# A two-layer hybrid diffusion step on one core: the first context pair's gate-up product moved to POOL, its down products placed ahead of the latent index list

## The chip, the cores and the metric

The kernel runs as one program on one core of a Trainium2 chip. The metric is device time in microseconds (us), median over runs. Engines: PE (TensorE, matmuls), DVE (VectorE), ACT (ScalarE), POOL (GpSimd) and SP (SyncE, which here only issues DMAs).

## The reference, cut to what matters

One step of a two-layer trunk for 128 context tokens and 512 latent tokens, model width 1024, float32. Each layer mixes tokens (attention, pooling, short convolution), adds a residual with a layer norm, and then runs a mixture of 16 experts of width 512, in which every expert picks its own tokens:

```python
def expert_choice_ffn(u, w_router, w_gate, w_up, w_down):
    B, T, D = u.shape
    cap = CAPACITY_FACTOR * T // N_EXPERTS
    aff = jax.nn.softmax((u @ w_router).astype(jnp.float32), axis=-1)
    g, idx = lax.top_k(aff.swapaxes(1, 2), cap)
    xs = jax.vmap(lambda ub, ib: ub[ib])(u, idx)
    hdn = (jax.nn.silu(jnp.einsum('becd,edf->becf', xs, w_gate))
           * jnp.einsum('becd,edf->becf', xs, w_up))
    ye = jnp.einsum('becf,efd->becd', hdn, w_down) * g[..., None].astype(u.dtype)
```

The two token sets are routed apart: an expert takes 16 of the 128 context tokens and 64 of the 512 latent ones. The rows of `ye` are then added back to their tokens.

## The kernel before, in words

The experts are worked in 8 pairs per layer (`NPAIR`). A pair has two kinds of rows: 2 x 16 context rows (in two blocks of 32) and 2 x 64 latent rows. Their products go into PSUM banks: `ps_gc` holds gate and up of the context rows, in four blocks of 32 partitions (gate and up of the first expert, gate and up of the second); `ps_g` and `ps_u` hold those of the latent rows; `ps_dc` and `ps_d` the down products.

A pair's context part is a chain: `context` (matmuls into `ps_gc`), `ctx_hidden` (ACT takes Silu of the gate block into `sc`, DVE multiplies it with the up block in PSUM into `hc`, once per expert), `ctx_turn` (PE transposes `hc` into `ps_hcT`, ACT copies that to `hcT`), `ctx_rows` (32 matmuls into `ps_dc`, then DVE scales the rows into `yc`), `scatter` (POOL adds `yc` to the accumulator `yaccc` by indirect DMA).

The first pair (j == 0) is special, since the latent tokens are not chosen yet when it begins. `route_late` finishes the router for the last latent tile with context matmuls filled in between (`fill`), picks the 64 best tokens per expert on DVE (`topk`: eight rounds of max, replace, find index), and builds the index list (`route_lat`): DVE writes `ldup`, PE transposes it (`tcol`, into `ps_tc`), DVE casts it to `lgi`, and POOL gathers the first pair's rows `xsl` from DRAM with `lgi` (`gather`). A second list, of the weights, goes the same way (`lvd`, `lg`). PE then transposes `xsl` (`turn_x`), ACT and DVE turn it into `xT`, and `ps_g`, `ps_u` follow.

The order of each engine's queue comes from a scheduler that emits instructions as it finds them ready. `tc.issue_after(x)` puts what follows behind `x` in that order; between engines it makes no wait at run time. `mm` and `turn1` chain most expert matmuls and transposes to each other in this way (`line["pe"]` is the last of them, line 239 issues them all). Before, the two DVE multiplies of the first pair's `ctx_hidden` were put behind the cast of `lgi`:

```python
scatter(yaccc, ctx_rows(ctx_turn(ctx_hidden(order["lgi"]))), csi, j)
```

Two more things hang on the gather. The weight tiles of 1 MB (`wg`, `wu`, `wd`) come through SP's queue into 16 buffers, refilled as PE frees them. Load number 13 (`GATE`, the tile `wg_3_0`) is held until POOL has written one element of its buffer, and that memset stands behind the first gather:

```python
if n == GATE:
    with tc.issue_after(order["gather"].ins):
        nc.gpsimd.memset(t[0:1, 0, 0:1], 0.0)
```

And POOL applies the layer norm's gain and bias to the latent residual tiles (lines 337 and 338, about 2.4 us each) and stores them to `yacc` (line 842); these stand in its queue around the gathers. The last 6 of the 96 weight tiles of a layer are paced: each waits until the one two places before it has landed (`PACED`, `PACE`).

Of the kernel before, what the change touches and what calls it, by code (L numbers as in the profile page):

```python
# [16 lines left out]
ALU = mybir.AluOpType  # L17
# [18 lines left out]
CAPL = 64  # L36
# [29 lines left out]
def kernel(ctx: ExitStack, tc: tile.TileContext, a: dict):  # L66
    nc = tc.nc
# [9 lines left out]
    order = {}  # L77
# [77 lines left out]
    yaccc = dram.tile([CROWS, EDIM], F32, name="yaccc")  # L155
# [78 lines left out]
    line = {}  # L234
# [541 lines left out]
    def out_proj(l, mixA, mixC, w2, ms, mixed):  # L776
# [170 lines left out]
        def route_late(fill):  # L947


            ins = turn(3, 1, fill(2), lambda ins: fill(1, ins))  # L950
            route(3, fill(1, ins))
            fill(9, order["weighed"])
            latr = route_lat(rt, rx, topk(rx, afl, CAPL, "ta"))
            order.pop("gather", None)
            x_first = gather(newrow("xsl"), zrow[:, :], latr[0][:, 0:1])
            cpool(f"rx{l}")
            return latr, x_first
# [98 lines left out]
    def experts(l, A, B, ctxr, ln, gates, newrow, newhalf, residual, xc, route_late, ps_dn, preload, start_next, finish, keep):  # L1056
# [68 lines left out]
        for j in range(NPAIR):  # L1125
# [34 lines left out]
            def ctx_hidden(after=None):  # L1160
                sc = newhalf("sc")
                hc = newhalf("hc")[0:64]
                for i in range(2):
                    nc.scalar.activation(out=sc[64 * i + 32:64 * i + 64], in_=pc[64 * i:64 * i + 32], func=AF.Silu)  # L1164
                    with tc.issue_after(after.ins) if after else ExitStack():
                        nc.vector.tensor_tensor(out=hc[32 * i:32 * i + 32], in0=pc[64 * i + 32:64 * i + 64],  # L1166
                                                in1=sc[64 * i + 32:64 * i + 64], op=ALU.mult)
                return hc
# [9 lines left out]
            def ctx_rows(hcT, pd=None):  # L1178
                if pd is None:
                    pd = ps_dn.tile("ps_dc")  # L1180
                for f in range(4):
                    for q in range(4):
                        i, n = q // 2, q % 2
                        mm(pd[32 * q:32 * q + 32, :], lhsT=hcT[:, f, 32 * i:32 * i + 32],
                           rhs=w["d", i, f // 2][:, f % 2, n * 512:n * 512 + 512], start=(f == 0), stop=(f == 3))
                yc = newhalf("yc") if j == NPAIR - 1 else wk.tile([P, 512], F32, tag="yc", name="yc", bufs=2)
# [33 lines left out]
            if j == 0:  # L1220
# [7 lines left out]
                (lgi, lso, lg, llast), x_first = route_late(fill)  # L1228
                xp = opool(f"xT{l}", "left")
                scatter(yaccc, ctx_rows(ctx_turn(ctx_hidden(order["lgi"]))), csi, j)  # L1230
# [320 lines left out]
```

## Time and profile before

| | |
|---|---|
| median of 3 runs | 1268.43 us (1268.24 to 1269.1) |
| profiled execution, its own time | 1264.65 us |
| its span in the trace | 1262.9 us |
| PE busy | 1180.2 us, 93% of the span |
| DVE, ACT, POOL busy | 542.2, 367.9, 252.6 us |
| mean DMA rate over the span | 271 GB/s |

Times in the trace count from the start of the span. Layer 0's selection of latent tokens lies at 349 to 361 us, its expert stage runs to about 640 us; layer 1's selection lies at 947 to 959 us. A timeline row gives start, duration, engine, line, operation, output and inputs, partitions x elements, count, and in brackets how long the engine was idle before and what ended that. A busy PE is one with a matmul in flight, at whichever of its two clocks (1.2 or 2.4 GHz); the granted clock is 0.5 or 1.0 in the rows by stretch.

### The profile page before, as it was taken

Reading aid. Unit: us, or ns where it says so; the run is one execution under the profiler, and the core shown is the slowest. Engines: PE = TensorE matmul, PEld = TensorE weight load, DVE = VectorE, ACT = ScalarE, POOL = GpSimd, SP = SyncE. Lnnn points to the kernel's source line nnn. Section 1 sums busy time; section 2 is a strip of 40 time slices with the busy share of each in tenths; the row PEclk is TensorE's granted clock in tenths of the full one; section 3 lists DMA queues with packets and bytes.
Section 4 is the critical chain, followed back from the end, with each engine's and each line's share of the span. In section 5 each row is a group of like instructions: output and inputs, shape, how many; then the busy total and the mean of one; then the engine's idle time right before and its main releaser. Section 6 shows DMA issues by size and latency. Waiting matters only on the chain.

```text
span 1262.9 us, 18196 instructions
## 1 busy us (share of the span) xinstructions
PE 1180.2 (93%) x7244; PEld 707.2 (56%) x7244; DVE 542.2 (43%) x1266; ACT 367.9 (29%) x800; POOL 252.6 (20%) x234
## 2 busy tenths in 40 slices
PE   5999999999959999999979999999996999999994
PEld 1877786987623333333349999698762333333331
DVE  1555454786551121111187656477644111111126
ACT  1532234672411111111155423466341111111111
POOL 0210001003241211112165100100324121112304
PEclk9999999999989999999989999999998999999997
DMA  9858674353869999999943324425396999999972
GB/s 365 309 205 315 220 268 175 127 175 135 328 235 404 402 397 409 408 407 362 327 142 96 78 60 201 168 100 194 132 341 236 402 399 402 410 408 406 358 252 84
DMA packets 85078, 342.34 MB, mean 271 GB/s; under 512 B 18713, under 2 KB 32089, under 8 KB 54401
## 3 DMA queue, kind: packets, MB, share of 16 engines
q1 hardware_dynamic: 73568, 305.96, 62.6%
q0 software_dynamic: 9840, 29.45, 8.5%
q10 hardware_dynamic: 1584, 5.77, 1.1%
q8 instruction: 57, 0.93, 0.3%
q14 instruction: 29, 0.23, 0.1%
HBM read 313.73 MB, written 27.51 MB: 270 GB/s over the span
## 4 chain that ended last, share of the span: by engine, by line
PE 83%; DVE 7%; DMA 4%; ACT 3%; issue 1%; SPq 0%; POOL 0%; POOLq 0%; ACTq 0%; DVEq 0%
PE ps_d L239 9%; PE ps_g L239 8%; PE ps_u L239 8%; PE ps_gc L239 8%; PE ps_dc L239 4%; PE ps_ada L185 4%; PE ps_c L230 3%; PE ps_c L232 3%; PE ps_c L231 3%; PE ps_o L231 3%; PE ps_o L230 3%; PE ps_o L232 3%; DMA r_wA<-in_w_in_dram 1%; PE tr L239 1%; PE ps_p L733 1%
## 5 line engine op out<-in xcount | busy, mean ns | idle before, releaser
L239 PE MATMUL ps_d<-wd,hT 128*64 128x512 f32 x512 | 114.9, 596 | 5.0 <-DVE yc L1187 3.2
L239 PE MATMUL ps_g<-wg,xT 128*64 128x512 f32 x512 | 116.1, 595 | 0.1
L239 PE MATMUL ps_u<-wu,xT 128*64 128x512 f32 x512 | 115.3, 592 | 0.0
L239 PE MATMUL ps_gc<-wu,xc 128*32 128x512 f32 x512 | 115.0, 594 | 0.0
L239 PE MATMUL ps_gc<-wg,xc 128*32 128x512 f32 x512 | 115.0, 594 | 0.0
L1164 ACT ACTIVATE sc<-ps_gc 32x512 f32<-32x512 f32 x32 | 18.8, 588 | 304.7 <-PE ps_gc L239 276.3
L1166 DVE TENSOR_TENSOR hc<-ps_gc,sc 32x512 f32<-32x512 f32 x32 | 22.0, 688 | 175.0 <-ACT sc L1164 174.9
L239 PEld LDWEIGHTS ps_d<-wd,hT 128*64 128x64 f32 x512 | 35.9, 137 | 82.1 <-issue 77.2
L239 PEld LDWEIGHTS ps_g<-wg,xT 128*64 128x64 f32 x512 | 36.0, 137 | 75.2 <-issue 70.1
L239 PEld LDWEIGHTS ps_u<-wu,xT 128*64 128x64 f32 x512 | 37.2, 137 | 72.6 <-issue 72.6
L239 PEld LDWEIGHTS ps_gc<-wg,xc 128*32 128x32 f32 x512 | 29.2, 110 | 75.0 <-issue 74.0
L1215 DVE SCALAR_TENSOR_TENSOR ye<-ps_d,lg,gl 128x512 f32<-128x512 f32 x32 | 24.0, 751 | 99.7 <-PE ps_d L239 99.7
L185 PE MATMUL ps_ada<-wada,cs 128*32 128x512 f32 x368 | 60.2, 631 | 4.9 <-DMA wada<-in_w_ada_dram 4.8
L239 PE MATMUL ps_dc<-wd,hcT 128*32 128x512 f32 x512 | 61.0, 618 | 0.9 <-ACT hcT L1175 0.9
L1113 POOL DMA_INDIRECT yaccc<-yc,csi x28 | 39.7, 1418 | 104.1 <-DVE yc L1187 75.5
L1194 DVE TENSOR_TENSOR h<-ps_u,sg 128x512 f32<-128x512 f32 x16 | 11.1, 692 | 104.0 <-PE ps_u L239 104.0
L961 POOL DMA_INDIRECT xsl<-zrow,lgi x16 | 15.9, 994 | 167.5 <-PE tr L239 152.9
L261 ACT ACTIVATE xT<-tr,modB,modA 128x128 f32<-128x128 f32 x64 | 27.8, 457 | 27.1 <-DVE xT L264 26.6
L1113 POOL DMA_INDIRECT yacc<-ye,lgi x14 | 19.9, 1418 | 76.9 <-DVE ye L1215 44.4
L285 POOL TENSOR_TENSOR bsd<-bsd,neg_half 128x1 f32<-128x1 f32 x15 | 9.5, 636 | 127.8 <-DVE bsd L284 127.8
L239 PEld LDWEIGHTS ps_dc<-wd,hcT 128*32 128x32 f32 x512 | 15.4, 113 | 34.6 <-issue 31.8
L227 POOL TENSOR_TENSOR wo00l<-r_wo,wo00h 128x1024 fp32r<-128x1024 f32 x4 | 10.4, 2614 | 119.4 <-ACT wo00h L226 119.4
(616 smaller groups left out, 2828.8 us busy)
## 6 DMA issues: line engine op xcount, KB each, us to landing
wg<-in_w_gate_dram SPq DMA_DIRECT2D x64, 1024.0 KB
wu<-in_w_up_dram SPq DMA_DIRECT2D x64, 1024.0 KB
wd<-in_w_down_dram SPq DMA_DIRECT2D x64, 1024.0 KB
wada<-in_w_ada_dram SPq DMA_DIRECT2D x46, 1024.0 KB
r_wo<-in_w_out_dram SPq DMA_DIRECT2D x8, 1024.0 KB
zrow<-xa ACTq DMA_DIRECT2D x8, 512.0 KB
yacc<-xa POOLq DMA_DIRECT2D x8, 512.0 KB, 11.2
z<-yacc SPq DMA_DIRECT2D x8, 512.0 KB
```

What stands on the lines that cost most here:

```text
L185: nc.tensor.matmul(ps[32 * j:32 * j + 32, :], lhsT=cs[:, k, :], rhs=w[:, j * 512:(j + 1) * 512], start=(k == 0), stop=(k == KD - 1))
L230: nc.tensor.matmul(out, lhsT=lh, rhs=rh, start=first, stop=False)
L231: nc.tensor.matmul(out, lhsT=lh, rhs=rl, start=False, stop=False)
L232: nc.tensor.matmul(out, lhsT=ll, rhs=rh, start=False, stop=last)
L239: line["pe"] = op(*args, **kw)
L261: nc.scalar.activation(out=out[:, kk, :], in_=ps[:, kk, :], func=AF.Identity, scale=A[:, r, k:k + 1], bias=B[:, r, k:k + 1])
L733: nc.tensor.transpose(pt[:, kk, i * P:(i + 1) * P], prs[i][:, (k0 + kk) * P:(k0 + kk + 1) * P], ident)
L961: ins = nc.gpsimd.indirect_dma_start(out=x, out_offset=None, in_=src, in_offset=bass.IndirectOffsetOnAxis(ap=idx, axis=0))
L1113: nc.gpsimd.indirect_dma_start(out=acc[:, :], out_offset=bass.IndirectOffsetOnAxis(ap=idx[h][0:64, j:j + 1], axis=0), in_=y[hs], in_offset ...
L1164: nc.scalar.activation(out=sc[64 * i + 32:64 * i + 64], in_=pc[64 * i:64 * i + 32], func=AF.Silu)
L1166: nc.vector.tensor_tensor(out=hc[32 * i:32 * i + 32], in0=pc[64 * i + 32:64 * i + 64], in1=sc[64 * i + 32:64 * i + 64], op=ALU.mult)
L1215: order["ye"] = nc.vector.scalar_tensor_tensor(out=ye[:, hs], in0=pd, scalar=lg[:, j:j + 1], in1=gl2[:, hs], op0=ALU.mult, op1=ALU.mult)
```

## The change

`ctx_hidden` of the first pair now works without DVE: ACT first copies both up blocks out of PSUM into `uc`, then takes the two Silus, and POOL multiplies `uc` with `sc`. The down products are split from their scaling (`ctx_sums`, `ctx_scaled`). `route_late` calls `down` (hidden, turn and down products of the first pair) between `topk` and `route_lat`, and `route_lat` is put behind the last down product in the issue order. The scaling of the rows stands behind the cast of `lgi`. The same is done in both layers; pairs 1 to 7 keep their order.

```diff
-        def route_late(fill):
+        def route_late(fill, down):
...
             fill(9, order["weighed"])
-            latr = route_lat(rt, rx, topk(rx, afl, CAPL, "ta"))
+            best = topk(rx, afl, CAPL, "ta")
+            pd = down()
+            with tc.issue_after(line["pe"].ins):
+                latr = route_lat(rt, rx, best)
             order.pop("gather", None)
             x_first = gather(newrow("xsl"), zrow[:, :], latr[0][:, 0:1])
...
-            def ctx_hidden(after=None):
+            def ctx_hidden(pool=False):
                 sc = newhalf("sc")
                 hc = newhalf("hc")[0:64]
+                uc = newhalf("uc") if pool else None
                 for i in range(2):
+                    u = pc[64 * i + 32:64 * i + 64]
+                    if pool:
+                        u = uc[64 * i + 32:64 * i + 64]
+                        nc.scalar.copy(out=u, in_=pc[64 * i + 32:64 * i + 64])
+                for i in range(2):
+                    u = (uc if pool else pc)[64 * i + 32:64 * i + 64]
                     nc.scalar.activation(out=sc[64 * i + 32:64 * i + 64], in_=pc[64 * i:64 * i + 32], func=AF.Silu)
-                    with tc.issue_after(after.ins) if after else ExitStack():
-                        nc.vector.tensor_tensor(out=hc[32 * i:32 * i + 32], in0=pc[64 * i + 32:64 * i + 64],
-                                                in1=sc[64 * i + 32:64 * i + 64], op=ALU.mult)
+                    (nc.gpsimd if pool else nc.vector).tensor_tensor(out=hc[32 * i:32 * i + 32], in0=u,
+                                                                     in1=sc[64 * i + 32:64 * i + 64], op=ALU.mult)
                 return hc
...
-                (lgi, lso, lg, llast), x_first = route_late(fill)
+                def down():
+                    return ctx_sums(ctx_turn(ctx_hidden(True)), ps_dn.tile("ps_dc"))
+
+                (lgi, lso, lg, llast), x_first, pd = route_late(fill, down)
                 xp = opool(f"xT{l}", "left")
-                scatter(yaccc, ctx_rows(ctx_turn(ctx_hidden(order["lgi"]))), csi, j)
+                with tc.issue_after(order["lgi"].ins):
+                    yc = ctx_scaled(pd)
+                scatter(yaccc, yc, csi, j)
```

On PE, layer 0, behind the last context matmul of the first pair (first row; - is before, + the changed kernel; `ldup` and `lvd` are the index and weight lists):

```order
 L239 MATMUL ps_gc<-wu_1_1_3607,xc_2880 32x512
-L989 MATMUL ps_tc<-ident,ldup 128x16
-L989 MATMUL ps_tc<-ident,lvd 128x16
 L239 MATMUL ps_hcT<-ident,hc 128x64 x4
 L239 MATMUL ps_dc<-wd_0_0_3609,hcT 32x512 x2
@@ -1570,6 +1568,8 @@
 L239 MATMUL ps_dc<-wd_0_1_3613,hcT 32x512 x2
 L239 MATMUL ps_dc<-wd_1_1_3615,hcT 32x512 x2
-L239 MATMUL tr_3778<-ident,xsl 128x128 x4
-L239 MATMUL tr_3787<-ident,xsl 128x128 x4
+L992 MATMUL ps_tc<-ident,ldup 128x16
+L992 MATMUL ps_tc<-ident,lvd 128x16
```

The two list transposes stood directly behind the last context matmul; now the four transposes of `hc` and all 32 down products (eight such rows, of four each) stand ahead of them. Behind them come the transposes of `xsl`, as before.

On POOL, layer 0, from the last small reciprocal root of the router to the weight gate (the memset on `wg_3_0`), before:

```order
L285 TENSOR_TENSOR bsd<-bsd,neg_half 128x1
L337 TENSOR_TENSOR xa<-xa,ln_g_2885 128x1024
L338 TENSOR_TENSOR xa<-xa,ln_b_2888 128x1024
L961 DMA xsl<-zrow,lgi 128x1024
L337 TENSOR_TENSOR xa<-xa,ln_g_2885 128x1024
L961 DMA xsl<-zrow,lgi 128x1024
L1074 MEMSET wg_3_0_3895 1x1
L842 DMA yacc<-xa 128x1024
```

and in the changed kernel:

```order
L1175 TENSOR_TENSOR hc<-uc,sc 32x512 x2
L337 TENSOR_TENSOR xa<-xa,ln_g_2885 128x1024
L338 TENSOR_TENSOR xa<-xa,ln_b_2888 128x1024
L842 DMA yacc<-xa 128x1024
L964 DMA xsl<-zrow,lgi 128x1024
L337 TENSOR_TENSOR xa<-xa,ln_g_2885 128x1024
L964 DMA xsl<-zrow,lgi 128x1024
L1077 MEMSET wg_3_0_3898 1x1
```

The two products stand ahead of the residual tile's gain and bias, and one store to `yacc` has moved ahead of the first gather.

On ACT, layer 0, from the router's last exponential to the first piece of `xT`, in the changed kernel:

```order
L904 ACTIVATE rex,rsm<-rex,rmx 128x16
L1171 COPY uc<-ps_gc 32x512 x2
L1174 ACT_TABLE_LOAD
L1174 ACTIVATE sc<-ps_gc 32x512 x2
L1184 COPY hcT<-ps_hcT 128x256
L261 ACTIVATE xT<-tr_3781,modB_2896,modA_2895 128x128
```

The table load stood directly behind that exponential and ahead of the first Silu; it has moved behind the two copies, which wait for PE's last context matmul.

## Rows read from the trace of the kernel before

**Rows 1.** The page, shares of the span in the chain that ended last.
```profile
PE 83%; DVE 7%; DMA 4%; ACT 3%; issue 1%; SPq 0%; POOL 0%; POOLq 0%; ACTq 0%; DVEq 0%
```

**Rows 2.** Timeline of PE, layer 0, first pair (columns as above).
```profile
351.99 0.59 PE L239 MATMUL ps_gc<-wu,xc 128*32 128x512 f32 x1
360.46 0.28 PE L989 MATMUL ps_tc<-ident,ldup 16*128 16x16 f32 x1 [7.88 <-DVE ldup L1036]
...
364.01 0.71 PE L239 MATMUL ps_hcT<-ident,hc 64*128 64x64 f32 x4 [1.81 <-DVE hc L1166]
365.18 5.12 PE L239 MATMUL ps_dc<-wd,hcT 128*32 128x512 f32 x32 [0.46 <-ACT hcT L1175]
370.23 1.24 PE L239 MATMUL tr<-ident,xsl 128*128 128x128 f32 x8
```

**Rows 3.** Timeline of PE, down products of the second pair, layer 0.
```profile
418.06 3.64 PE L239 MATMUL ps_dc<-wd,hcT 128*32 128x512 f32 x32
```

**Rows 4.** Timeline of PE, layer 1, first pair.
```profile
963.01 4.88 PE L239 MATMUL ps_dc<-wd,hcT 128*32 128x512 f32 x32 [0.46 <-ACT hcT L1175]
967.82 1.24 PE L239 MATMUL tr<-ident,xsl 128*128 128x128 f32 x8
```

**Rows 5.** Timeline of POOL, layer 0, around the first gather.
```profile
352.32 2.34 POOL L338 TENSOR_TENSOR xa<-xa,ln_b 128x1024 f32<-128x1024 f32 x1
361.41 1.05 POOL L961 DMA_INDIRECT xsl<-zrow,lgi  x1 [6.76 <-DVE lgi L1041]
...
365.99 0.09 POOL L1074 MEMSET wg<- 1x1 f32 x1
...
369.33 0.57 POOL L842 DMA_DIRECT2D yacc<-xa  x1 [0.30 <-POOL xa L338]
```

**Rows 6.** Instructions on `xsl`, 955 to 962 us: layer 1's first gather alone.
```profile
DMA to landing us min/median/max: 4.5/4.5/4.5
```

**Rows 7.** Timeline of ACT, layer 0, two copies, table load, first Silu.
```profile
343.46 1.08 ACT L883 COPY u<-tr 128x512 f32<-128x512 f32 x2
...
348.03 0.19 ACT L904 ACTIVATION_READ_ACCUMULATOR rex<-rex,rmx 128x1 f32 x1
348.23 1.28 ACT L1164 ACT_TABLE_LOAD   x1
352.65 0.59 ACT L1164 ACTIVATE sc<-ps_gc 32x512 f32<-32x512 f32 x1 [3.13 <-PE ps_gc L239]
```

**Rows 8.** Groups of POOL by form (busy, mean ns, idle before).
```profile
L1470 POOL TENSOR_TENSOR z<-z,ln_g 128x384 f32<-128x384 f32 x3 | 3.6, 1190 | 4.6 <-ACT z L1462 4.6
...
L227 POOL TENSOR_TENSOR wB00l<-r_wB,wB00h 128x640 fp32r<-128x640 f32 x2 | 3.1, 1570 | 5.3 <-ACT wB00h L226 5.3
```

**Rows 9.** Timeline of DVE, layer 0, the second multiply.
```profile
363.17 0.69 DVE L1166 TENSOR_TENSOR hc<-ps_gc,sc 32x512 f32<-32x512 f32 x1 [0.28 <-ACT sc L1164]
```

**Rows 10.** By stretch: length, busy per engine, granted clock, DMA share, GB/s.
```profile
357.50:358.00 0.50, 0.00 (x0) 0.00 (x0) 0.50 (x3) 0.00 (x0) 0.00 (x0) 0.98 0.00 0
368.00:368.50 0.50, 0.50 (x8) 0.09 (x4) 0.00 (x0) 0.00 (x0) 0.50 (x1) 0.78 0.78 98
400.00:420.00 20.00, 20.00 (x142) 7.33 (x142) 3.95 (x8) 3.80 (x9) 1.41 (x1) 1.00 1.02 398
```

**Rows 11.** Timeline of PE, last pair's down products, layer 0, then layer 1.
```profile
621.24 5.36 PE L239 MATMUL ps_d<-wd,hT 128*64 128x512 f32 x22 [0.26 <-DMA wd<-in_w_down_dram]
1215.77 7.09 PE L239 MATMUL ps_d<-wd,hT 128*64 128x512 f32 x32
```

**Rows 12.** Timeline of SP, the last pair's four `wd` loads, layer 0, then layer 1.
```profile
602.50 12.22 SPq L1077 DMA_DIRECT2D wd<-in_w_down_dram  x4
1199.75 11.44 SPq L1077 DMA_DIRECT2D wd<-in_w_down_dram  x4
```

**Rows 13.** Timeline of ACT at the start: a table load and what follows it.
```profile
3.25 1.28 ACT L147 ACT_TABLE_LOAD   x1 [3.25 <-DMA craw<-in_c_ctx_dram]
4.55 0.22 ACT L147 ACTIVATE cs<-craw 128x16 f32<-128x16 f32 x1
```

More of the change, by code (lines that the diff above doesn't have):

```diff
@@ L956, in route_late @@
             cpool(f"rx{l}")
-            return latr, x_first
+            return latr, x_first, pd
         return A, B, ctxr, ln, gates, newrow, newhalf, residual, xc, route_late, ps_dn
@@ L1178, in ctx_rows, with ctx_sums @@
             def ctx_rows(hcT, pd=None):
-                if pd is None:
-                    pd = ps_dn.tile("ps_dc")
+                return ctx_scaled(ctx_sums(hcT, pd or ps_dn.tile("ps_dc")))
+            def ctx_sums(hcT, pd):
                 for f in range(4):
@@ L1185, in ctx_rows, with ctx_scaled @@
                            rhs=w["d", i, f // 2][:, f % 2, n * 512:n * 512 + 512], start=(f == 0), stop=(f == 3))
+                return pd
+            def ctx_scaled(pd):
                 yc = newhalf("yc") if j == NPAIR - 1 else wk.tile([P, 512], F32, tag="yc", name="yc", bufs=2)
```

## The prediction

> **What bounds the kernel now.** I read the page first, then PE's timeline around the first pair, then the queues of ACT, POOL and SP beside it. The chain that ended last is 83% PE [rows 1], so a microsecond counts only where PE stands still or runs at its low clock. The selection of latent tokens is such a place. PE's last context matmul of the first pair ends at 351.99 + 0.59 = 352.58; the index list's transpose starts at 360.46, after 7.88 us without work [rows 2]. Then come the parts that the change moves: the transposes of `hc` at 364.01, the down products from 365.18 for 5.12 us, and only behind them, at 370.23, the transposes of the gathered rows `xsl` [rows 2]. The reader should see two things. The gather was not the last wait: POOL issued it at 361.41 [rows 5], and layer 1's landed 4.5 us after its issue [rows 6], so layer 0's rows were there at about 365.9, 4.3 us ahead of 370.23. PE's down products filled that time. And the 5.12 us are half cold: the same 32 matmuls take 3.64 us in the next pair [rows 3], because the granted clock fell from 2.4 to 1.2 GHz just ahead of 358.0, 5.4 us after PE's last matmul, and rose at about 368.2, 3.0 us after the down products began [rows 10]. Layer 1 shows the same pattern 597.8 us later, with 4.88 us for the down products [rows 4].
>
> So up to 4.3 us a layer could be won if all of the context chain fitted under the selection. Whether it fits decides the sign.
>
> **Step 1, the chain under the selection (layer 0).** It starts when ACT sees the last context matmul, at 352.65 [rows 7]. ACT copies two 32x512 blocks; two copies of 512 columns took 1.08 us [rows 7]. The table load for Silu, 1.28 us [rows 7], used to run at 348.23 while ACT waited for PE and cost nothing; behind the copies its cover is gone and it counts in full. The first Silu takes 0.59. That makes 352.65 + 1.08 + 1.28 + 0.59 = 355.60; the second Silu runs beside POOL's first product. POOL's product with 512 columns is not in the trace. From below it is bounded by DVE's 0.69 [rows 9], from above by POOL's own 2.34 for 1024 columns [rows 5]; its forms of 384 and 640 columns took 1.19 and 1.57 [rows 8], and I take their middle, 1.38, since 512 lies half-way. With 0.15 us for a hand-over between engines (DVE's multiply ended at 363.86 and PE went on at 364.01 [rows 9, 2]), the two products end at 355.75 + 2.76 = 358.51. PE starts on `hc` at 358.66. From there to the first down product took 365.18 - 364.01 = 1.17 us [rows 2], so that starts at 359.83. PE has then been idle for 6 us, longer than the 5.4 after which the clock fell, so I take 5.12 and not 3.64: the end is at 364.95 (363.47 at full clock).
>
> **Step 2, the wait that is added.** The index list is ready for PE at 360.46 as before, since DVE's queue ahead of it is the same. But its transpose now stands behind all 32 down products in PE's queue, so it starts at 364.95, 4.49 us late. Behind it wait DVE's cast, POOL's gather, and behind the gather POOL's second gather and the memset that lets the weight stream go on. The change says that the down products run while the tokens are selected; by this sum 0.6 us of them do. The gather is issued at 361.41 + 4.49 = 365.90. POOL does not hold it longer: from 358.51 the residual tile's gain and bias take some 2.34 each, then the store that has moved ahead of the gather 0.30 + 0.57 [rows 5], which is 364.1. The rows land 4.5 us later, at 370.4, against 370.23 before: +0.2. The bounds of the landing are 4.5 and 5.8, if the store's 512 KB, 1.3 us at 398 GB/s [rows 10], had to go first; I take 4.5, since that store is issued 2 us earlier into queues that stood idle (share 0.00 ahead of 358 [rows 10]). The 6.2 us of context work gone from between are paid for by the later gather.
>
> **Step 3, the clock.** Before, PE came to `xsl` from the down products, with its clock up. Now it stands from 364.95 to 370.4, 5.4 us with only two short list transposes in them, which is the time after which the clock fell before. The latent matmuls then start at 1.2 GHz. The price is bounded by 0 and by what the low clock cost the down products, 5.12 - 3.64 = 1.48 [rows 2, 3]; I take 1.48. PE's path in layer 0: 0.2 + 1.5 = +1.7. In layer 1 the down products take 4.88, the wait is 4.25 and everything else the same: +1.6.
>
> **Step 4, the weight stream.** The memset at 365.99 [rows 5] moves with the gather, by 4.5 us, and the stream of 1 MB tiles starts again that much later. The store that moved ahead uses 1.3 us of this idle time, so 3.2 us of stream are lost in layer 0 and 2.9 in layer 1. From 370 us on the queues are full (share 1.02, 398 GB/s [rows 10]). In layer 0 PE waited 0.26 us for the last `wd` tiles, so there is no slack; in layer 1 it did not wait [rows 11]. Layer 1's last `wd` load was issued by 1211.2, 596.5 us behind layer 0's at 614.7 [rows 12], while PE's first pairs lie 597.8 apart: its stream is 1.3 us ahead. If the delay is carried to the end, layer 0 ends 3.2 and not 1.7 late (+1.5), and layer 1 2.9 - 1.3 = 1.6, as late as PE is anyway. If the queues catch up within 200 us, nothing is added. The ends are 0 and 1.5; neither is nearer, and I take 0.8.
>
> **The sum.** 1.7 + 1.6 + 0.8 = **+4.1 us**: 1264.65 + 4.1 = 1268.75 for the profiled execution. The median of the runs shown is 1268.43, 3.8 above that execution; against it the forecast is 1272.5. DVE loses two multiplies of 0.69 and ACT gains 1.08 of copies, both off PE's path otherwise. A change under 0.2%, 2.5 us, is about what a measurement here cannot tell from none.
>
> **A rule beside a row.** ACT's table load shows 1.28 us, with the instruction before it ending at 348.22 and the load starting at 348.23 [rows 7]; at the start of the kernel the next activation follows 0.02 us after a load [rows 13]. The Trainium skill (ScalarE: Activation LUTs, What ACT_TABLE_LOAD costs) gives about 1283 ns for the load and some 1380 ns more for a drain at every switch of table. The trace agrees with the first figure and shows none of the second at these two places. By the page the sum would be +6.9; it is the last rival.
>
> **The rivals.**
> *Faster: the chain fits better.* If POOL's products take 0.69 each and the down products run at full clock, these end at 363.47 - 1.38 = 362.1, the rows land at 367.5, and the clock, idle for 5.4 us again, may hold: -2.7 a layer, -5.4 in all, 1263.0. It decides at the end of the down products: ahead of 363.3 the change wins even with a cold clock, ahead of 364.8 with a warm one. For it speaks only that the clock fell just 5.4 us after PE's last matmul; against it, that POOL takes 1.19 for even 384 columns [rows 8]. Chance 0.09.
> *No change: the clock stays up once.* Where it falls depends on moments that differ between executions. If the down products run warm or the latent matmuls do, a layer ends between -1.3 and +0.2, and the stream adds up to 1.5: about +0.5 in all, 1268.9. Chance 0.24.
> *Much slower: the stream decides.* If the store brings nothing and the full 4.5 us reach both ends, less 1.3 in layer 1: 4.5 + 3.2 = +7.7, 1276.1. For it: PE's wait of 0.26 us with full queues [rows 10, 11]. Chance 0.10.
> *The drain counts.* An extra 1.4 us between ACT's copies and its Silus delays everything by as much in each layer: 4.1 + 2.8 = +6.9, 1275.3. No row shows it. Chance 0.05.
>
> **How the numbers follow.** The forecast has 0.52; a tenth of that lies under +2.5. Slower by over 0.2%: 0.47 + 0.10 + 0.05 = 0.62. Within 0.2%: 0.05 of the forecast and 0.22 of the no-change case, 0.27. Faster: 0.09 and the rest of that case, 0.02, so 0.11. The range runs from -1.4 (a layer won at -1.3) to +9.6 (the much slower case and 1.9 more, the landing's 1.3 a layer in part): 1267.0 to 1278.0, leaving out most of the faster case and little above.
>
> **What would show it.** In the profile after: ACT's table load between the copies and the first Silu; POOL's products at about 1.4 us; the first down product near 359.8 and the list's transpose idle for nothing but PE's own queue until about 365; the gather issued near 365.9 and `xsl` transposed near 370.4; the first `ps_g` group slower than its neighbours; the memset on `wg` near 370.5; a longer wait for `wd` at layer 0's end. The prediction is wrong if the list's transpose starts within 2 us of 360.5, or if `xsl` is transposed ahead of 368.5 with the clock up.

## The result, and the profile after

The changed kernel takes 1286.45 us (median, 1281.62 to 1288.01) against 1268.76 of the kernel before on the same chip: ratio 1.0129, 95% interval 1.0099 to 1.0159, slower by 17.7 us. The profiled execution took 1286.75 us with a span of 1284.9, 22.1 us over that of before. The forecast was +4.1.

The page's shares of the chain that ended last [rows 1], and three rows of PE's waits (in all, times, longest), both of the changed kernel:

```profile
PE 66%; DMA 14%; issue 9%; DVE 4%; ACT 3%; POOL 3%; SPq 0%; POOLq 0%; ACTq 0%; DVEq 0%
```

```profile
PE ps_z L1318 <- DMA z<-yacc: 12.3, 1, 12.3
PE ps_hcT L239 <- POOL hc L1175: 11.8, 2, 5.9
...
PE tr L239 <- DMA xsl<-zrow,lgi: 7.3, 2, 3.8
```

DMA went from 4% to 14% of the chain. The second and third wait were forecast; the first, 12.3 us on the tiles `z`, was not. It lies at the end of layer 1, far from the edit.

PE's timeline around the first pair of layer 0, after (answers to [rows 2]):

```profile
358.84 0.73 PE L239 MATMUL ps_hcT<-ident,hc 64*128 64x64 f32 x4 [5.90 <-POOL hc L1175]
360.04 6.30 PE L239 MATMUL ps_dc<-wd,hcT 128*32 128x512 f32 x32 [0.46 <-ACT hcT L1184]
366.27 0.23 PE L992 MATMUL ps_tc<-ident,ldup 16*128 16x16 f32 x1
367.70 0.20 PE L992 MATMUL ps_tc<-ident,lvd 16*128 16x16 f32 x1 [1.20 <-DVE lvd L1052]
371.41 1.98 PE L239 MATMUL tr<-ident,xsl 128*128 128x128 f32 x8 [3.51 <-DMA xsl<-zrow,lgi]
373.32 4.80 PE L239 MATMUL ps_g<-wg,xT 128*64 128x512 f32 x16
```

The order is the forecast one: down products, list, wait for the gather, then latent rows at a low clock. How far behind PE is, is read from fixed points: the transposes of `hc` in the second pair, and the start of each layer's selection (start of PE's first instruction behind the context matmuls, less its idle time). Before, then after, from PE's timelines:

```profile
415.80 0.69 PE L239 MATMUL ps_hcT<-ident,hc 64*128 64x64 f32 x4
...
958.29 0.28 PE L989 MATMUL ps_tc<-ident,ldup 16*128 16x16 f32 x1 [7.89 <-DVE ldup L1036]
...
1013.38 0.69 PE L239 MATMUL ps_hcT<-ident,hc 64*128 64x64 f32 x4
```

```profile
419.42 0.69 PE L239 MATMUL ps_hcT<-ident,hc 64*128 64x64 f32 x4
...
625.91 5.36 PE L239 MATMUL ps_d<-wd,hT 128*64 128x512 f32 x22 [1.31 <-DMA wd<-in_w_down_dram]
...
960.33 0.74 PE L239 MATMUL ps_hcT<-ident,hc 64*128 64x64 f32 x4 [5.88 <-POOL hc L1175]
...
1020.12 0.69 PE L239 MATMUL ps_hcT<-ident,hc 64*128 64x64 f32 x4
```

| point on PE | before | after | behind |
|---|---|---|---|
| layer 0, selection starts | 352.58 | 352.94 | 0.36 |
| layer 0, `hcT` of the second pair | 415.80 | 419.42 | 3.62 |
| layer 0, second part of the last `ps_d` [rows 11] | 621.24 | 625.91 | 4.67 |
| layer 1, selection starts | 950.40 | 954.45 | 4.05 |
| layer 1, `hcT` of the second pair | 1013.38 | 1020.12 | 6.74 |
| layer 1, last pair's `ps_hT` | 1214.10 | 1236.81 | 22.71 |
| end of the span | 1262.9 | 1284.9 | 22.0 |

The two first pairs cost 3.3 and 2.7 us. Sixteen of the 22 us arise between the last two rows of PE. Its order there, first before, then after (the left number is the place in PE's queue):

```
4482 L239 MATMUL ps_hT<-ident,h 128x128 x4
4515 L239 MATMUL ps_z<-z_10103,ident 128x512
4516 L1300 MATMUL ps_z<-z_10106,ident 128x512 x2
```

```
4482 L1318 MATMUL ps_z<-z_10112,ident 128x512 x2
4483 L239 MATMUL ps_hT<-ident,h 128x128 x4
4516 L239 MATMUL ps_z<-z_10109,ident 128x512
```

Two matmuls that bring tile 2 of the residual into `ps_z` (line 1318, in `join`) have moved ahead of the whole last pair. They are among the few of this stage that `mm` does not chain, so the scheduler may put them anywhere. And they need `z`, which SP can load only behind POOL's last scatter to `yacc`. PE's timeline of that place, after, and three stretches of the table by stretch (columns as in [rows 10]):

```profile
1233.23 3.78 PE L1318 MATMUL ps_z<-z,ident 128*128 128x512 f32 x4 [12.32 <-DMA z<-yacc]
1236.81 1.06 PE L239 MATMUL ps_hT<-ident,h 128*128 128x128 f32 x4
...
1239.49 7.09 PE L239 MATMUL ps_d<-wd,hT 128*64 128x512 f32 x32
```

```profile
1222.00:1226.00 4.00, 0.00 (x0) 0.00 (x0) 0.00 (x0) 0.00 (x0) 0.00 (x0) 0.95 0.73 283
1226.00:1230.00 4.00, 0.00 (x0) 0.00 (x0) 0.00 (x0) 0.00 (x0) 0.00 (x0) 0.50 0.95 324
...
1233.00:1237.00 4.00, 3.77 (x5) 1.59 (x6) 0.00 (x0) 0.00 (x0) 0.00 (x0) 0.50 0.11 46
```

PE stands for 12.32 us and then starts at 1.2 GHz. POOL's last scatters of layer 1, before and after, show why `z` is late as well:

```profile
1192.43 1.40 POOL L1113 DMA_INDIRECT yaccc<-yc,csi  x1 [2.11 <-DMA yaccc<-yc,csi]
1197.97 1.41 POOL L1113 DMA_INDIRECT yacc<-ye,lgi  x1 [4.13 <-DVE ye L1215]
1199.89 1.40 POOL L1113 DMA_INDIRECT yaccc<-yc,csi  x1 [0.51 <-DMA yaccc<-yc,csi]
1203.92 1.41 POOL L1113 DMA_INDIRECT yacc<-ye,lso  x1 [2.63 <-DMA yacc<-ye,lgi]
```

```profile
1198.84 1.40 POOL L1116 DMA_INDIRECT yaccc<-yc,csi  x1 [2.46 <-DMA yaccc<-yc,csi]
1205.94 1.40 POOL L1116 DMA_INDIRECT yaccc<-yc,csi  x1 [5.70 <-DMA yaccc<-yc,csi]
1207.64 1.40 POOL L1116 DMA_INDIRECT yacc<-ye,lgi  x1 [0.30 <-issue]
1216.52 1.40 POOL L1116 DMA_INDIRECT yacc<-ye,lso  x1 [7.48 <-DMA yacc<-ye,lgi]
```

The first `yacc` scatter now queues behind a `yaccc` scatter that waits 5.70 us for the one before it to land. The last one is issued 12.6 us later than before, where the pair itself is 6.74 late. So the sentence above that pairs 1 to 7 keep their order was wrong: it holds in the source, but not for PE at the end of layer 1, nor for POOL at the end of either layer. In the pairs between, a gather on POOL and some copies on ACT and DVE also changed places with their neighbours; these small moves stay in every kernel below that is built on the change, and no run takes them back.

One more thing was not foreseen: two small DVE instructions took ten times as long. DVE and POOL, layer 0, the end of the selection, after:

```profile
359.39 1.87 DVE L1034 COPY tlv<-tav 16x64 f32<-16x64 f32 x1
...
361.40 2.37 DVE L1036 TENSOR_TENSOR tkeep<-tav,tlv 16x64 uint32<-16x64 f32 x1
...
364.41 0.22 DVE L1039 COPY ldup<-tlf 16x128 f32<-16x128 f32 x1
```

```profile
356.20 2.59 POOL L1175 TENSOR_TENSOR hc<-uc,sc 32x512 f32<-32x512 f32 x2 [13.87 <-ACT sc L1174]
358.87 2.35 POOL L337 TENSOR_TENSOR xa<-xa,ln_g 128x1024 f32<-128x1024 f32 x1
361.30 2.40 POOL L338 TENSOR_TENSOR xa<-xa,ln_b 128x1024 f32<-128x1024 f32 x1
...
367.16 1.00 POOL L964 DMA_INDIRECT xsl<-zrow,lgi  x1 [2.55 <-DVE lgi L1044]
...
371.71 0.09 POOL L1077 MEMSET wg<- 1x1 f32 x1
```

Before, the same copy and comparison took 0.18 and 0.20 us. Now each ends within 0.1 us of POOL's gain or bias beside it, and the list is ready at 364.6 instead of 360.4. PE's down products hide this until 366.27.

### The profile page after: what moved, and what is told of

Read it like the earlier page. It is cut to its first block, busy times and chain, and to the rows that moved or that the text cites. A ratio compares the mean times of both kernels' runs of the same rounds, so it can differ in the third digit from the quotient of the medians.

```text
span 1284.9 us, 18200 instructions
## 1 busy us (share of the span) xinstructions
PE 1190.9 (93%) x7244; PEld 711.5 (55%) x7244; DVE 545.3 (42%) x1262; ACT 369.7 (29%) x804; POOL 257.5 (20%) x238
## 4 chain that ended last, share of the span: by engine, by line
PE 66%; DMA 14%; issue 9%; DVE 4%; ACT 3%; POOL 3%; SPq 0%; POOLq 0%; ACTq 0%; DVEq 0%
PE ps_d L239 5%; PE ps_gc L239 5%; PE ps_g L239 4%; PE ps_u L239 4%; PE ps_ada L185 4%; PE ps_c L230 3%; PE ps_c L232 3%; PE ps_c L231 3%; PE ps_o L231 3%; PE ps_o L230 3%; PE ps_o L232 3%; DMA yaccc<-yc,csi 2%; DMA yacc<-ye,lso 2%; DMA wg<-in_w_gate_dram 2%; PE ps_dc L239 2%
## 5 line engine op out<-in xcount | busy, mean ns | idle before, releaser
L1175 DVE TENSOR_TENSOR hc<-ps_gc,sc 32x512 f32<-32x512 f32 x28 | 19.3, 688 | 174.0 <-ACT sc L1174 174.0
L239 PE MATMUL ps_dc<-wd,hcT 128*32 128x512 f32 x512 | 63.2, 638 | 0.9 <-ACT hcT L1184 0.9
L264 DVE TENSOR_SCALAR xT<-tr,modA,modB 128x128 f32<-128x128 f32 x64 | 24.9, 408 | 26.0 <-PE tr L239 15.4
```

What stands on the lines that cost most here:

```text
L239: line["pe"] = op(*args, **kw)
L264: nc.vector.tensor_scalar(out=out[:, kk, :], in0=ps[:, kk, :], scalar1=A[:, r, k:k + 1], scalar2=B[:, r, k:k + 1], op0=ALU.mult, op1=ALU.add)
L1175: (nc.gpsimd if pool else nc.vector).tensor_tensor(out=hc[32 * i:32 * i + 32], in0=u, in1=sc[64 * i + 32:64 * i + 64], op=ALU.mult)
```

## The experiments

In the diffs below `...` stands for lines left out.

**Which of the two ends, and how much the first pair.** Four kernels. In a1, PE's order alone is taken back:

```diff
-        context(range(5, KD))
+        order["rest"] = context(range(5, KD))
...
-                put(ps, lhsT=ident, rhs=zs[t][:, cols], start=True, stop=False)
+                with tc.issue_after(order["rest"].ins) if t == 2 else ExitStack():
+                    put(ps, lhsT=ident, rhs=zs[t][:, cols], start=True, stop=False)
```

> The changed kernel with one thing taken back: the two matmuls that bring tile 2 of the residual into ps_z at the end of layer 1 stand behind the last context matmul again, as before the change; POOL's scatter order stays changed. Theory (PE's order at the end of layer 1): of the +22.0 us between the two profiled executions, 15.97 arise between 1220 and 1237 us, where PE stood 12.32 us before these two matmuls with 93 expert matmul rows queued behind them, and then ran cold. Back in their old place they are reached at about 1233.2 us, when their tile has just landed (1233.2), so the wait goes: about 16 us less than the changed kernel, some 1270 to 1273 us, +3 to +6 on the kernel before, and no wait of over 1 us for z. Rival (scatters): the reordered scatters make z late whatever PE does; then PE waits at the new place instead and at most 5 us come back, 1281 or more. Rival (first pair): the loss was made in the first pairs and the end only shows it: no change, 1286.

In a2, POOL's scatters alone are taken back (`scatter` got an argument that names its halves; a line left out issues the first half of `yc` where both stood):

```diff
...
-            if j < NPAIR - 1:
+            if j == NPAIR - 2:
+                first = scatter(yacc, ye, lso, j, (0,))
+                with tc.issue_after(first.ins):
+                    second = scatter(yaccc, yc, csi, j, (1,))
+                with tc.issue_after(second.ins):
+                    scatter(yacc, ye, lso, j, (1,))
+            elif j < NPAIR - 1:
                 scatter(yacc, ye, lso, j)
```

> The changed kernel with POOL's last scatters of each layer in the order of before (the first yacc scatter ahead of the second yaccc scatter); PE's order at the end stays changed. Theory (PE's order): the two early ps_z matmuls still wait for z, but z comes sooner: in the kernel before the third z load landed 1221.1, which with this kernel's shift of 6.74 is 1227.9 against 1233.2. So PE's wait for z shrinks from 12.3 to about 7 us and the time falls by some 5 us, to about 1281. Rival (scatters are the whole of it): the time falls by 12 to 16 us, to 1270 to 1274. Rival (first pair): no change.

a3 has both edits, and b1 is the kernel before with the two matmuls put early (the loads of `z` are written down with them, but SP issues them in the order of before):

> The changed kernel with both taken back: PE's two ps_z matmuls and POOL's last scatters stand as before the change. What is left is the edit in the first pair of each layer alone. Theory (PE's order): equal to the kernel with only PE's order back within 1 us, since z lands there just when it is needed; +3 to +6 us on the kernel before. From the trace of the changed kernel the first pairs leave 3.3 us (layer 0) + 1.0 (wd wait at layer 0's end) + 2.7 (layer 1), less what ends at the tail, about 6. Rival (scatters): clearly faster, by 3 us or more, than the kernel with only PE's order back. My blind sum for this part was +4.1.

```diff
                 context(range(4))
+                if l + 1 == a["depth"]:
+                    load_zs()
+                    for n in range(2):
+                        early.append(ptr("ps_z"))
+                        mm(early[n], lhsT=ident, rhs=zs[2][:, n * 512:n * 512 + 512], start=True, stop=False)
                 hT = lat_transpose(h)
...
```

> The kernel before with nothing of the change but its accident: the two ps_z matmuls of tile 2 at the end of layer 1 are put ahead of the last pair's ps_hT transposes. Theory (PE's order): PE reaches them at 1214.1 us, their tile lands at 1221.1, so PE waits 7.0 us and then runs cold for a few us: +8 to +11 us on the kernel before, some 1277 to 1280. Rival (first pair): PE loses nothing that it would not lose anyway, within 2 us of the kernel before.

| kernel | median us | ratio to before | interval |
|---|---|---|---|
| the change | 1286.45 | 1.0129 | 1.0099 to 1.0159 |
| a1, PE's order back | 1275.33 | 1.0073 | 1.0058 to 1.0089 |
| a2, scatters back | 1280.30 | 1.0105 | 1.0087 to 1.0124 |
| a3, both back | 1271.06 | 1.0042 | 1.0026 to 1.0058 |
| b1, before with PE's order early | 1275.18 | 1.0063 | 1.0044 to 1.0083 |

Each ratio goes by the kernel before as run in the same round (medians of 1266.1 to 1268.8, and for c1, c2, c3 and d1 below on another chip), so ratios are compared and not medians.

The rival that the first pair makes the loss is out: a3 keeps the whole edit of the first pair and loses 0.0042 of 1267 us, 5.3, where the change loses 0.0129, 16.4 (17.7 by the medians). PE's order is the larger part, but a1 missed its 1270 to 1273. Its trace says why: the wait for `z` is gone, and PE waits for the last `wd` tiles in both layers instead (a1 twice, then a3's only one):

```profile
626.72 5.36 PE L239 MATMUL ps_d<-wd,hT 128*64 128x512 f32 x22 [1.72 <-DMA wd<-in_w_down_dram]
...
1227.65 5.36 PE L239 MATMUL ps_d<-wd,hT 128*64 128x512 f32 x22 [1.94 <-DMA wd<-in_w_down_dram]
```

```profile
1223.46 5.37 PE L239 MATMUL ps_d<-wd,hT 128*64 128x512 f32 x22 [0.37 <-DMA wd<-in_w_down_dram]
```

So the scatter order has a price of its own. That the late scatters hold up the last weight loads by running beside them fits this, but no run shows it. That I had taken the two kernels for equal was wrong. a2 came as expected, with PE's wait for `z` at 7.3 us. b1 is 8.0 us above the kernel before by its ratio, the low end of the +8 to +11 expected (its median lies below the 1277 to 1280 given with it). In its trace, which is of the slowest of its executions, PE waited 9.27 us for `z` and not 7.0.

**The ends without the change.** b2 is the kernel before with the scatter order of the change, b3 adds the early matmuls. The edit of b2:

```diff
-                scatter(yaccc, ctx_rows(hcT), csi, j)
+                order["cs"] = scatter(yaccc, ctx_rows(hcT), csi, j)
...
-                scatter(yacc, ye, lso, j)
+                with tc.issue_after(order["cs"].ins) if j == NPAIR - 2 else ExitStack():
+                    scatter(yacc, ye, lso, j)
```

> The kernel before with one accident of the change: in both layers POOL's last yaccc scatter stands ahead of the last pair's first yacc scatter, as in the changed kernel; PE's queue and the first pair are untouched. Theory (two accidents at the layers' ends): the yacc scatters come 3 to 5 us later and run beside the last wd loads, PE waits for wd some 1.5 us longer in each layer, as it did with only PE's order taken back (1.72 and 1.94 against 0 and 0.37): +2 to +4 us on the kernel before. Rival (the scatter order matters only behind a first pair that is late): within 1 us of the kernel before.

> The kernel before with both accidents, and nothing else of the change: PE's two ps_z matmuls early at the end of layer 1, and the scatter order of the changed kernel in both layers. Theory (two accidents at the layers' ends): this makes the most of the loss. From the changed kernel's +17.7 and the +5 of the kernel with both ends back: +11 to +14 us on the kernel before, 1278 to 1281, with a wait of about 12 us for z ahead of the early ps_z matmuls. Rival (the accidents only cost that much behind a late first pair): no more than with PE's order alone, +8.

b2 took 1269.11 us, ratio 1.0021 (1.0007 to 1.0035), +2.7 us; its profiled execution, one of the faster ones (1267.59), waited only 0.6 us for `wd`, so the size is as expected and the way it comes about is not shown. b3 took 1280.86, ratio 1.0102 (1.0088 to 1.0115), +12.9 us as expected, with PE's wait at 9.43 where about 12 were expected:

```profile
1229.01 3.78 PE L239 MATMUL ps_z<-z,ident 128*128 128x512 f32 x4 [9.43 <-DMA z<-yacc]
```

With nothing of the change's purpose in it, b3 makes the larger part of the loss. With a3's 5.3 us the two parts give 18.2, against 16.4 with an interval of 12.6 to 20.2 for the change: the account closes within that interval.

**What the first pair's parts cost.** All built on a3. In c1 ACT takes each Silu ahead of its copy:

```diff
-                for i in range(2):
...
-                        nc.scalar.copy(out=u, in_=pc[64 * i + 32:64 * i + 64])
...
-                    nc.scalar.activation(out=sc[64 * i + 32:64 * i + 64], in_=pc[64 * i:64 * i + 32], func=AF.Silu)
+                    act = nc.scalar.activation(out=sc[64 * i + 32:64 * i + 64], in_=pc[64 * i:64 * i + 32], func=AF.Silu)
+                    if pool:
+                        with tc.issue_after(act.ins):
+                            nc.scalar.copy(out=u, in_=pc[64 * i + 32:64 * i + 64])
```

> Built on the kernel with both ends back. One edit: in the first pair ACT takes each Silu ahead of the copy of its up block, so the table load stands behind the router's last exponential again, where ACT waits for PE anyway. Theory (the table load lies on the chain): POOL's first product needs one Silu and one copy, 0.59 + 0.54 us behind PE's last context matmul, instead of 1.08 + 1.28 + 0.59; so hcT, the down products and the list's transpose come 1.8 us sooner, and the rows of the latent tokens too: 1.8 us a layer, 3.6 in all against the kernel with both ends back (1271.1), about 1267.5. Rival (the list itself is late, held up on DVE by POOL's two residual instructions): PE is free 1.8 us sooner but waits for the list, and under 1 us a layer comes back, 1269.5 or more.

c2, built on c1, puts the list ahead of the down products (and the weight list behind them); c3, built on c2, takes POOL's residual tiles out of the way (with POOL's products held behind the store of tile 1); d1, built on a3, fills PE's wait:

```diff
...
-            pd = down()
-            with tc.issue_after(line["pe"].ins):
-                latr = route_lat(rt, rx, best)
+            hcT = turned()
+            latr, pd = route_lat(rt, rx, best, lambda: down(hcT))
...
```

> Built on c1_silu_first. The index list's transpose stands ahead of the 32 down products in PE's queue (behind the transposes of hc), the weight list's transpose behind them; the store of the residual tile falls behind the gather. Theory (DVE is held up by POOL): POOL runs the residual's gain and bias in about 358 to 363 us, beside DVE's copy into tlv and the comparison into tkeep, which take some 1.9 and 2.4 us instead of 0.18 and 0.20 as in the changed kernel; so the list is ready near 363.2 and not 360.5, the down products behind it start late, and the time is that of c1_silu_first within 1.5 us. Rival (the stretch of the two DVE instructions was an accident of that place): list at 360.5, latent rows transposed near 366.5, 3 us a layer less than c1_silu_first.

```diff
             best = topk(rx, afl, CAPL, "ta")
+            residual(1)
...
-                for t in (1, 2, 3):
-                    residual(t, order["last"].ins if t == 3 else None)
+                for t in (2, 3):
+                    residual(t, order["last" if t == 3 else "gather"].ins)
...
```

> Built on c2_list_first. POOL's gain and bias on latent tile 1 stand ahead of its two products (where they stood before the change), those on tiles 2 and 3 behind the first gather, so POOL has nothing to do while DVE builds the index list. Theory (DVE is held up by POOL): tlv and tkeep take 0.2 us each again, the list is transposed near 360.6 us, the gather is issued near 361.6 and lands near 366, the down products end near 366, and the latent rows are transposed some 3.5 to 4 us sooner than in the kernel before in both layers: about 5 to 8 us below the kernel before, 1259 to 1262. Rival (the weight stream or the clock takes it back): the first pair is done sooner, but the end of the layer waits for wd, and the whole stays within 2 us of the kernel before.

```diff
+                with tc.issue_after(order["tcol"].ins):
+                    for i in range(6):
+                        mm(pg, lhsT=ident, rhs=w["g", 0, 0][:, i % 4, :], start=True, stop=True)
                 xs0 = load_x(0)
```

> Built on the kernel with both ends back. Between the list's transposes and the transposes of the latent rows PE runs 6 matmuls whose result nobody reads (128x128 by 128x512 into ps_g, overwritten later), about 2.7 us warm, inside its 3.7 us wait for the gather. Theory (the clock): with work in that wait the eight transposes take 1.24 us instead of 1.99 and the first ps_g group 3.65 instead of 4.5 to 5.6: 1.5 to 2.5 us a layer, 3 to 5 in all, about 1266.5 to 1268. Rival (the clock is low for the down products' sake, whatever PE does in the wait): no gain, or up to 1 us a layer lost because the fillers outlast the wait.

Executions differ by some us before the selection begins, so the first pair is read from PE's timeline as above: from the start of the selection to the second pair's `hcT`.

| kernel | median us | ratio (interval) | first pair, layer 0 | layer 1 |
|---|---|---|---|---|
| before | | | 63.2 | 63.0 |
| the change | 1286.45 | 1.0129 | 66.5 | 65.7 |
| a3 | 1271.06 | 1.0042 | 65.5 | 65.4 |
| c1 | 1268.62 | 1.0010 (0.9995 to 1.0026) | 64.6 | 62.5 |
| c2 | 1271.19 | 1.0030 (1.0015 to 1.0045) | 63.9 | 62.4 |
| c3 | 1270.23 | 1.0028 (1.0013 to 1.0043) | 59.5 | 60.0 |
| d1 | 1273.91 | 1.0057 (1.0039 to 1.0076) | 67.5 | 65.8 |
| c5 (below) | 1270.37 | 1.0029 (1.0012 to 1.0046) | 68.8 | 59.6 |
| c6 (below) | 1264.77 | 0.9981 (0.9969 to 0.9993) | 59.7 | 59.4 |

c1: 0.9 and 2.8 us come back, 1.9 on average for the 1.8 expected. PE's wait for `hc` fell from 5.9 us in a3 to 4.0 in both layers, so the table load, together with one of the two copies, lay on the chain. What else sets the layers apart is the down products (5.34 and 5.17 us, for 4.86 and 5.79 in a3) and, in layer 0, a wait for the gather of 4.33 us for 3.79. The time is 1268.62 for the 1267.5 expected.

c2 gains little more in the first pair, and c3 shows the reason. Its median is 2.6 us above c1's, outside the 1.5 us expected. In layer 0 its trace has one more wait of 1.6 us for DVE's `yc` than c1's, and one of 1.07 us for ACT's `xT`; the rest stays open. The same DVE rows of c2, with the row between them and POOL's beside them, then of c3, where POOL has nothing to do at that time:

```profile
360.16 0.18 DVE L1033 COPY tlv<-tav 16x64 f32<-16x64 f32 x1
360.37 2.22 DVE L985 CAST taf<-tai 48x64 f32<-48x64 uint32 x1
362.51 0.21 DVE L1035 TENSOR_TENSOR tkeep<-tav,tlv 16x64 uint32<-16x64 f32 x1
...
360.16 2.38 POOL L338 TENSOR_TENSOR xa<-xa,ln_b 128x1024 f32<-128x1024 f32 x1
```

```profile
361.49 0.18 DVE L1034 COPY tlv<-tav 16x64 f32<-16x64 f32 x1
361.70 0.19 DVE L986 CAST taf<-tai 48x64 f32<-48x64 uint32 x1
361.81 0.20 DVE L1036 TENSOR_TENSOR tkeep<-tav,tlv 16x64 uint32<-16x64 f32 x1
```

In c2 POOL's gain ended at 360.08, and the copy fell into the gap before the bias. So neither the copy nor the comparison is held, as was expected, but the cast between them: 2.22 us for 0.19, until POOL's bias ends at 362.54. From copy to comparison it takes 2.35 us there and 0.32 in c3, and PE has the list 10.0 us behind the start of the selection in c2, 8.0 in c3 and 7.9 in the kernel before. In the first pair c3 is 3.7 and 3.0 us shorter than before, where 3.5 to 4 were expected. But its time was expected at 1259 to 1262, and is 1270.23: PE waits 6.0 us for `wd` in it, 3.88 of them at layer 0's end, and 1.6 us for DVE's `yc` four times, where the kernel before has two such waits.

d1 lost 1.9 us against a3 by the ratios. Its fillers took 5.42 us and not 2.7 and outlasted the gather; in layer 1 they made the latent rows 2.0 us late, of which 1.7 came back. In layer 0 PE also waited 1.84 us for ACT's `xT`, ahead of which the scaling of the next layer norm's gain had moved. What the fillers warmed is there all the same, in layer 1's PE rows of d1 against 1.93 and 4.51 in a3:

```profile
971.00 5.42 PE L239 MATMUL ps_g<-wg,ident 128*128 128x512 f32 x12
976.26 1.12 PE L239 MATMUL tr<-ident,xsl 128*128 128x128 f32 x8
977.39 3.65 PE L239 MATMUL ps_g<-wg,xT 128*64 128x512 f32 x16
```

That is 0.81 + 0.86 = 1.7 us for the low clock behind the wait.

**Why a shorter first pair gives so little.** In c3 the memset that frees the weight stream stood 16.3 us behind the start of the selection (13.4 before). c5, built on c3, puts it earlier:

```diff
...
                 xs0 = load_x(0)
+                x_next = load_x(j + 1)
+                for e in (2, 3):
+                    ahead["g", e, 0] = eweight("g", e, 0)
...
-                    residual(t, order["last" if t == 3 else "gather"].ins)
+                    residual(t, order["opened"].ins)
```

> Built on c3_list_first_no_residual. POOL issues the second gather directly behind the first, then the memset that lets the weight stream go on, and only then the gains and biases of tiles 2 and 3; the first two weight loads of the second pair are written down earlier for that. In c3 the memset stood 16.3 us behind PE's last context matmul (13.4 in the kernel before), the first pair was 3.8 and 3.0 us shorter than before, and PE then waited 6.0 us for wd at the two ends. Theory (the weight stream, set free by that memset, took the gain back): the memset comes some 11.5 us behind PE's last context matmul, 2 us sooner than before, the waits for wd shrink to under 1 us, both layers stay 3 to 3.8 us shorter and the time is 1259 to 1262, 4 to 7 us under the kernel before. Rival (the stream is bound by its rate, not by its start): the waits for wd stay at 4 us or more and the time stays within 2 us of c3, 1268 to 1271. A second rival: two gathers one behind the other delay the first one's landing by 1 us or more, and the latent rows are transposed as late as before the change.

The medians of c5 and c3 do not differ, but the two layers do. In layer 0 ACT waited 10.74 us for the gain and 8.20 for the bias of the next layer norm, whose loads stand behind weight tiles in c5, and PE for ACT, 8.66 us. ACT's timeline of c5, the row of the bias, with which PE's wait ended:

```profile
392.52 1.06 ACT L333 ACTIVATE ln_b<-ln_b 128x1024 f32<-128x1024 f32 x1 [8.20 <-DMA ln_b<-in_ln_b_dram]
```

In layer 1 the first pair is 3.4 us shorter and the wait for `wd` down to 0.7. c6, built on c5, removes ACT's wait:

```diff
-                L2 = ln_params(ln, l, "ln2_g", "ln2_b", l + 1 < a["depth"])
+                with tc.issue_after(order["hT"].ins):
+                    L2 = ln_params(ln, l, "ln2_g", "ln2_b", l + 1 < a["depth"])
```

> Built on c5_gate_behind_gathers, where layer 0's first down products waited 8.7 us for ACT, which stood at the scaling of the next layer norm's gain, whose load had moved behind three weight tiles; here that scaling stands behind the second pair's hT on ACT. Theory (the weight stream ends the layer): the first pair of both layers is 3 to 4 us shorter than before, but layer 1 of c5 shows that with all of that PE only waits longer for the last wd tiles (from PE's last context matmul to the first ps_z 274.8 us against 275.1 before): so within 2.5 us of the kernel before, 1264 to 1268. Rival (the gain of the first pairs holds to the end): 6 to 7 us under the kernel before, 1260.

c6 takes 1264.77 us, 2.4 below the kernel before (interval 0.9 to 3.9) and the fastest kernel of the study. Its first pairs are 3.5 us shorter in both layers, and PE gives most of it back at the ends:

```profile
620.70 5.36 PE L239 MATMUL ps_d<-wd,hT 128*64 128x512 f32 x22 [1.41 <-DMA wd<-in_w_down_dram]
...
1215.91 5.36 PE L239 MATMUL ps_d<-wd,hT 128*64 128x512 f32 x22 [2.02 <-DMA wd<-in_w_down_dram]
```

From the start of the selection these are 267.9 and 268.0 us (352.85 and 947.89 in this execution). Before, PE was there after 621.24 - 352.58 = 268.7 in layer 0, with 0.26 us of wait, and after 267.6 in layer 1, with none. So first pairs 3.5 us shorter were worth 0.8 us at the end of layer 0 and nothing at the end of layer 1. Another 2.0 us of c6's lead over the kernel before lie from there to layer 1's selection (327.2 us for 329.2), in a stage that no edit meant to change; their cause is open. A later memset goes with a later end: in c3, with it at 16.3 us, the layers need 271.1 and 269.2 us to the same place. An earlier one brought little: at 11.7 instead of 13.4 c6 has the 0.8 us and nothing.

## Why the prediction was right and wrong

**Direction right, size 4 times too small.** The step that failed is the sum: "1.7 + 1.6 + 0.8 = +4.1". It has no term for a changed order of the queues at the ends of the layers: the prediction took the order behind the first pair for unchanged, and Step 4 priced the ends for the weight stream only. That left out PE's two unchained matmuls and POOL's late scatters: b3 measures them at +12.9 us without the first pair. The scheduled order of the queues at the ends of both layers is fixed before a run, and a term for it could have been made from the rows of the kernel before. No rival covered it; "much slower" put the price on the weight stream, and at +7.7 at most.

**Step 1, right.** Forecast: down products from 359.83; measured 360.04, of which 0.36 is this execution's lead-in. POOL's two products took 2.59 (2.76 forecast). The table load stood between copies and Silus and counted in full; c1 returned it together with one copy.

ACT's rows, after:

```profile
353.01 1.17 ACT L1171 COPY uc<-ps_gc 32x512 f32<-32x512 f32 x2 [4.43 <-PE ps_gc L239]
354.19 1.28 ACT L1174 ACT_TABLE_LOAD   x1
355.49 1.20 ACT L1174 ACTIVATE sc<-ps_gc 32x512 f32<-32x512 f32 x2
```

The load begins 0.01 us behind the copies and the Silu 0.02 behind the load, which rules out the rival of a drain. The Trainium skill (ScalarE: Activation LUTs, What ACT_TABLE_LOAD costs) gives about 1283 ns for the load, which these rows bear out, and some 1380 ns more for a drain with every switch to a different set, which they do not show.

**Step 2, right but for a size.** The down products were put at 5.12 us, and took 6.30 and 5.93 (4.86 and 5.79 in a3). PE comes to them with the clock low in the kernel before too; there it was granted low for about 3.0 us of them, in the changed kernel for about 5.4 and 4.7 us. So the list came at 366.27 for 364.95, the gather at 367.16 for 365.90, and the latent rows at 371.41 for 370.4. "The index list is ready for PE at 360.46 as before" was wrong by 4.2 us, without effect, as the list waited for PE anyway.

**Step 3, right.** 1.48 us forecast for the low clock behind the wait; in layer 0 the changed kernel shows 0.74 on the transposes (1.98 for 1.24) and 1.15 on `ps_g` (4.80 for 3.65 us in the kernel before), 1.89 in all, and in layer 1 it shows 1.55; d1 gave 1.7.

**Step 4, about right, by single executions.** 0.8 us, bounds 0 and 1.5. The table shows 1.05 more at layer 0's last `ps_d` in the changed kernel, but a1 and a3 assign such waits to the scatters at the end: with these back, PE waits 0.37 us in layer 1 and not at all in layer 0. So Step 4 is read from a3. Its first pairs are 2.3 and 2.4 us longer than before, and from the start of the selection it needs 2.0 and 3.3 us more to the second part of the last `ps_d`: 0.7 us in all beyond the first pairs.

With steps 1 to 4 alone, a3 is the kernel that was priced, but for the small moves in the pairs between: +5.3 us by its ratio, interval 3.3 to 7.3, for +4.1 forecast.

**The rivals.** No change and faster are out. "Faster" rested on a chain that ends ahead of the list. c3 and c6, which make the first pair as short as that or shorter, end 3.5 us above and 2.4 us below the kernel before; c6 also moves POOL's residual tiles, its second gather and the memset, and of its 2.4 at most 0.8 us lie in its expert stages.

## What to carry to other kernels

Where a scheduler sets the order, compare the order of every queue to the end of the program, not only around the edit, and look for the few instructions that nothing chains: one that waits for a late load holds up all that stands behind it. Before moving work into a wait, ask what ends the stage; here the last weight tile does, 268 to 269 us after the selection starts in the kernel before and in c6, and 271 in layer 0 of c3, where the weight stream was set free later. And when POOL gets work beside a chain of small DVE instructions, look at each of these again.

## What the runs showed of the hardware

DVE's copy (SBUF to SBUF, float32), its comparison with two SBUF inputs and, in c2, its cast stood still while POOL ran a 128x1024 product or sum (1.87, 2.37 and 2.22 us for 0.18, 0.20 and 0.19), while the maxima and index searches of the selection ran beside POOL's products at their usual pace (0.40 us a MAX8). The Trainium skill (SBUF — State Buffer, SBUF: two separate sides) names a pair of ports that a DVE instruction, in a 2-port mode or with two SBUF inputs, and a POOL instruction lock against each other for the whole instruction; c2 and c3 agree with it, though no row shows in which mode the copy and the cast ran.

A wait of 12.3 us left the clock at 1.2 GHz when PE went on (0.50 in the stretch 1233 to 1237), where the four rows of two matmuls took 3.78 us, against 1.88 for the same four in the kernel before (clock 1.00). Why the scheduler moved them was not tried.
